# Two-layer hybrid attention kernel: normalised x behind the last attention tile's casts, the last output tile in another PSUM bank, and seven scheduling constants

## The chip, the cores and the metric

The kernel runs on one core of a Trainium2 chip. The core has five engines that work side by side, each through its own queue in order: TensorE (PE, matmuls), VectorE (DVE), ScalarE (ACT), GpSimd (POOL) and SyncE (SP, which here only issues DMAs). They wait for one another through semaphores. Time is device microseconds of one execution; several executions are run and the median counts. All of the data is float32, and matmuls take it in a form called fp32r.

## The reference, cut to what matters

Two layers work on 1024 latent tokens and 256 context tokens of width 1024. Each one normalises x, scales and shifts it by a modulation, projects it, mixes it, and adds the gated projection back to x.

```python
for i in range(DEPTH):                       # DEPTH = 2
    sh_l, sc_l, g_l = modulation(c, mod_w[i], mod_b[i])
    h_lat = rms_norm(x_lat, norm_g[i]) * (1.0 + sc_l[:, None, :]) + sh_l[:, None, :]
    if i % 2 == 0:   # global attention (8 heads) and windowed attention (8 heads), silu gates, @ w_out
        y_lat, y_ctx = even_mixer(...)
    else:            # conformer convolution and 2-D neighbourhood attention (8 heads, bias table), @ w_out
        y_lat, y_ctx = odd_mixer(...)
    x_lat = x_lat + g_l[:, None, :] * y_lat
return rms_norm(x_lat, final_g)
```

## The kernel before

**Splits.** A float32 matmul is made of three fp32r products of a high and a low part: `mm3` (L362) issues hi·hi, lo·hi and hi·lo. `split` (L332) makes the parts: ACT casts the high part (L334), and POOL, or DVE where asked, subtracts to give the low part (L337). So each projection is a run of PE rows on L363, L364 and L365, and each operand costs a cast and a subtraction.

**Attention** is one generator, `attn_gen` (L453), used by both layers. Its work list has *groups* (in the first layer 4 sets of heads by 10 query blocks, in the second 16 pairs of head and half), and a group has *tiles* of 128 keys. A tile is: scores on PE into a bank `st` (L531, L535), exp on ACT into `pf` (L543; in the second layer most tiles add a bias table on DVE first, L540, then exp at L541), the split of `pf` into `ph` and `pl`, and three matmuls into the group's output bank `ov` (L472, L473, L474). The tag `ov` has one PSUM bank, so the first L472 of a group must wait until DVE has read the former group's output: two transposes (L482) and two multiplies (L700 in the first layer, L1546 in the second). Every `vshare`-th split gives its subtraction to DVE instead of POOL: `VS0 = 12` in the first layer, `VSH = 5` in the second.

Before a group's scores can start, its *prep* finds the row maxima: matmuls into `mx` banks (two of them; L645, L657, L665 in the first layer, L1520, L1528 in the second), a maximum on DVE, and a transpose (`trn`, L429) that gives the rows of `QL`. Prep number i+2 begins at the start of group i: it loads Q, and its steps are traced from `LEAD` tiles later on. In the second layer a new head's keys `KAt` (768 KB, L403) are loaded at the start of the head before, into the buffer that the head before that has just left.

**Fillers.** `weave` (L563) runs attention steps and, between them, steps of a second generator that keeps PE busy: the projections of the next set of heads, then its gates, then the output projection `po`. `NFILL`, `O1` and the literal counts say how many filler steps go with how many attention steps; `LAG` ties a filler to the scores of a tile some places back. The scheduler then orders each engine's instructions by priority and by its own estimate of when operands are ready, so a constant moves rows far from where it stands.

**The end of the first layer.** `through_attention` runs beside the last group's tiles: the output projection of the middle 512 tokens (`final_proj(1)`), and the first half of its normalisation `norm_h(1)`. `make_h` (L346) then takes, for each of eight 128-row pieces dk, x·scale·rstd on DVE (L351, rstd comes from PSUM as `bc`), and a high and a low part. Where the letter of `HV` for this piece is `v`, ACT adds the shift and rounds (L354) and DVE makes the low part (L355, `hl<-x,modT,hh`); where it is `g`, ACT adds the shift (L357) and casts (L334), and POOL subtracts (L337). After the attention come the projections of the context tokens (`po<-hc`, evicted on DVE at L1185) and the rest of the other chunk's, then the second layer's first projection.

**The second layer** has the convolution and its layer norm first, then the attention, with four fillers in turn: two head projections (`p`), the first half of the output projection (`po<-oc`, whose operands `oc` are split in `out1_alloc`, L1592, by DVE as `OCE` says), a quarter more of it (`po<-od`), and the last part with the final norm.

## Time and profile before

| | us |
|---|---|
| median of 3 runs | 1495.62 (1493.93 to 1496.02) |
| the profiled execution | 1491.75, of which span 1490.0 |
| PE busy | 1419.0 |
| DVE busy | 1069.9 |
| POOL busy | 821.8 |
| ACT busy | 739.1 |

A busy share is an average over stages. PE carries most of this span, so what can be won is in the stretches where PE stands still, and which instruction it stands before.

### The profile page before, as it was taken

What the parts mean: (1) busy time and instruction counts of PE and PEld (TensorE: products, weight loads), DVE (VectorE), ACT (ScalarE), POOL (GpSimd) and SP (SyncE); (2) the same over time, 40 slices, a digit from 0 to 9 for tenths busy, and PEclk for the clock granted to TensorE, in tenths of its full rate; (3) what the DMA queues carried; (4) which work ended last, traced back from release to release, by engine and by line L of the source; (5) the groups of instructions that cost most, each with busy time, mean ns of one, the idle gap of its engine ahead of it and who ended that gap; (6) DMA issues with size and microseconds to landing.
All of it is one profiled execution on the core that took longest, in us unless ns stands there. A gap on an engine that the chain in (4) does not pass through costs nothing.

```text
span 1490.0 us, 22025 instructions
## 1 busy us (share of the span) xinstructions
PE 1419.0 (95%) x7014; PEld 1146.4 (77%) x7014; DVE 1069.9 (72%) x2126; ACT 739.1 (50%) x1537; POOL 821.8 (55%) x802
## 2 busy tenths in 40 slices
PE   7899999999999999999999989999999999999996
PEld 2898978887888777677887768888777878777775
DVE  4687676588858786667756767999838566668757
ACT  3641453646355765665444645443434354545563
POOL 3561463657456786676554755764544343254673
PEclk9899999999999999999999999999999999999998
DMA  9675145314531235452221221214495867787623
GB/s 351 209 219 164 47 134 177 96 57 151 177 93 36 82 96 161 154 174 85 91 74 45 84 98 58 84 59 121 147 312 178 234 203 223 239 258 226 197 63 120
DMA packets 182922, 215.22 MB, mean 144 GB/s; under 512 B 17292, under 2 KB 136280, under 8 KB 182808
## 3 DMA queue, kind: packets, MB, share of 16 engines
q1 hardware_dynamic: 172560, 195.97, 42.2%
q10 hardware_dynamic: 10248, 17.87, 3.9%
q8 instruction: 55, 0.90, 0.3%
q14 instruction: 59, 0.48, 0.1%
HBM read 151.64 MB, written 62.13 MB: 143 GB/s over the span
## 4 chain that ended last, share of the span: by engine, by line
PE 74%; DVE 8%; DMA 7%; issue 4%; POOL 4%; ACT 2%; SPq 0%; DVEq 0%; POOLq 0%; ACTq 0%
PE p L363 7%; PE p L365 7%; PE p L364 7%; PE ov L472 4%; PE ov L474 4%; PE st L531 4%; PE ov L473 4%; PE st L535 4%; PE po L363 4%; PE po L365 3%; PE po L364 3%; PE pq L365 3%; PE pq L363 3%; PE pq L364 3%; PE pg L363 2%
## 5 line engine op out<-in xcount | busy, mean ns | idle before, releaser
L337 POOL TENSOR_TENSOR pl<-pf,ph 128x512 fp32r<-128x512 f32 (+3 forms) x321 | 391.6, 1235 | 263.8 <-ACT ph L334 213.4
L337 POOL TENSOR_TENSOR wl<-wr,wh 128x256 fp32r<-128x256 f32 (+2 forms) x253 | 193.9, 786 | 136.9 <-ACT wh L334 105.7
L543 ACT ACTIVATE pf<-st 128x512 f32<-128x512 f32 x284 | 165.6, 597 | 158.9 <-PE st L535 141.6
L334 ACT CAST ph<-pf 128x512 fp32r<-128x512 f32 (+3 forms) x364 | 204.3, 579 | 18.2 <-PE ov L473 8.6
L363 PE MATMUL p<-hh,wh 128*128 128x512 f32 x448 | 176.7, 396 | 3.5 <-ACT vT L1405 1.4
L364 PE MATMUL p<-hl,wh 128*128 128x512 f32 x448 | 177.2, 397 | 0.0
L365 PE MATMUL p<-hh,wl 128*128 128x512 f32 x448 | 174.2, 398 | 0.1
L334 ACT CAST wh<-wr 128x256 fp32r<-128x256 f32 (+2 forms) x260 | 100.8, 404 | 135.0 <-DMA wr<-in_od_d_dram 31.9
L472 PE MATMUL ov<-ph,Vt 128*97 128x512 f32 (+4 forms) x364 | 138.4, 381 | 12.7 <-DVE y L700 4.2
L474 PE MATMUL ov<-pl,Vt 128*97 128x512 f32 (+3 forms) x364 | 138.4, 381 | 5.2 <-POOL pl L337 2.6
L531 PE MATMUL st<-QH,KAt 128*128 128x512 f32 (+3 forms) x364 | 139.7, 385 | 2.5 <-ACT pf L543 0.9
L473 PE MATMUL ov<-ph,Vt 128*64 128x512 f32 (+3 forms) x364 | 135.9, 373 | 0.0
L535 PE MATMUL st<-QL,KBt 68*128 68x512 f32 (+3 forms) x364 | 134.6, 378 | 1.2 <-DVE QL L430 1.2
L658 DVE TENSOR_REDUCE mp<-mx 128x1 f32<-128x512 f32 x128 | 86.0, 683 | 57.6 <-PE mx L657 57.0
L1296 DVE SCALAR_TENSOR_TENSOR cps<-U,taps,cps 128x512 f32<-128x512 f32 x184 | 124.4, 747 | 0.0
L363 PEld LDWEIGHTS p<-hh,wh 128*128 128x128 f32 x448 | 84.2, 188 | 23.1 <-ACT wh L334 2.0
L365 PEld LDWEIGHTS p<-hh,wl 128*128 128x128 f32 x448 | 84.2, 188 | 20.7 <-POOL wl L337 1.0
L364 PEld LDWEIGHTS p<-hl,wh 128*128 128x128 f32 x448 | 84.2, 188 | 20.0 <-issue 0.5
L363 PE MATMUL pq<-wh,hh 128*128 128x384 f32 x256 | 88.6, 346 | 1.1 <-ACT pc L923 1.1
L365 PE MATMUL pq<-wh,hl 128*128 128x384 f32 x256 | 87.8, 344 | 1.8 <-POOL hl L337 1.8
L364 PE MATMUL pq<-wl,hh 128*128 128x384 f32 x256 | 88.3, 345 | 0.0
L472 PEld LDWEIGHTS ov<-ph,Vt 128*97 128x97 f32 (+1 forms) x364 | 60.9, 167 | 32.4 <-issue 8.2
(300 smaller groups left out, 3413.4 us busy)
## 6 DMA issues: line engine op xcount, KB each, us to landing
mw<-in_mod_w_dram SPq DMA_DIRECT2D x28, 512.0 KB, 5.9
Q<-qs SPq DMA_DIRECT2D x40, 256.0 KB, 2.7
QH<-Q SPq DMA_DIRECT2D x80, 128.0 KB, 2.8
bm<-in_d_bm_dram SPq DMA_DIRECT2D x16, 540.0 KB, 5.6
wr<-in_od_d_dram SPq DMA_DIRECT2D x64, 128.0 KB, 2.6
wr<-in_ev_qkv_dram SPq DMA_DIRECT2D x32, 192.0 KB, 4.5
QD<-spq SPq DMA_DIRECT2D x48, 128.0 KB, 2.5
KAt<-KD SPq DMA_DIRECT2D x8, 768.0 KB, 7.5
```

The source lines that it names most:

```text
L334: SC.copy(hi, src)
L337: (GP if leng == "g" else VE).tensor_tensor(lo, src, hi.bitcast(F32), op=ALU.subtract)
L363: PE.matmul(o, lh, rh, start=first, stop=False)
L364: PE.matmul(o, lh, rl, start=False, stop=False)
L365: done[0] = PE.matmul(o, ll, rh, start=False, stop=last)
L472: PE.matmul(o[0:m], V[:, vo + 64 : vo + 64 + m], ph, start=(t == 0), stop=False)
L473: PE.matmul(cut(g.ov[0:64], q0, n), V[:, vo : vo + 64], ph, start=False, stop=False)
L474: pvs.append(PE.matmul(o[0 : VW - 64], V[:, vo + 64 : vo + VW], pl, start=False, stop=(last and g.sink is None)))
L531: sts.append(PE.matmul(sf, KA[:, cs], cut(g.QH, q0, n), start=True, stop=False))
L535: PE.matmul(sf, KB[0:68, cs], cut(g.QL[0:68], q0, n), start=False, stop=True)
L543: SC.activation(pf[:, :n], st[:, :n], AF.Exp, scale=1.0 if g.bias else SCALE)
L1296: VE.scalar_tensor_tensor(pc, uc, w, pc, op0=ALU.mult, op1=ALU.add)
```

## The change

- `make_h` is cut in two. In the second layer's middle chunk, the high and low parts of pieces dk 5, 6 and 7 are issued behind the casts of the last attention tile: on each engine behind the last `cast` that it did there (ACT's `ph`, DVE's `pl`, POOL's `pl`). The order x·scale·rstd (L351) isn't bound.
- The first layer's last group takes its output bank from the tag `mx` (two banks) instead of `ov` (one).
- `HV` for the second layer: in the middle chunk piece 3 goes from g to v and piece 4 from v to g; in the last chunk piece 5 goes from v to g.
- `NFILL[2]` 34 to 37: the last set's projection runs ahead by three filler steps in 34. `O1[1]` 134 to 137: the first output projection is spread over three more attention steps, and the end of the layer has three fewer.
- `VSH` 5 to 7: a group of the second layer has seven tiles, so DVE now makes the low part of the last tile of every group, and no other.
- `OCE` v to g: the eight `oc` subtractions go from DVE to POOL.
- `LAG` (0, 0, 6, 12) to (0, 0, 3, 18). `LEAD` for the second layer 4 to 7, which delays the traced steps of a prep by three tiles.
- `AHEAD` 3 to 4 and `XA` 4 to 8: the function that `AHEAD` calls is empty in both layers, and with either value of either constant the instruction order is the same.

```diff
-LEAD = (3, 4)
-AHEAD = 3
+LEAD = (3, 7)
+AHEAD = 4
-VSH = 5
+VSH = 7
-OCE, ODE, OHE = ('v', 'g', 'g')
+OCE, ODE, OHE = ('g', 'g', 'g')
-LAG = (0, 0, 6, 12)
+LAG = (0, 0, 3, 18)
-NFILL = (34, 34, 34)
-HV = (('gggvvvvg',) * 3, ('gggvvvvg', 'vvvgvvvg', 'gggvvvvg'))
-O1 = (6, 134, 14)
+NFILL = (34, 34, 37)
+HV = (('gggvvvvg',) * 3, ('gggvvvvg', 'vvvvgvvg', 'gggvvgvg'))
+O1 = (6, 137, 14)
-XA = 4
+XA = 8
...
+    cast = [None] * 3
+    tailc = [None] * 3
     def split(src, hi, lo, heng="s", leng="g"):
         if heng == "s":
-            SC.copy(hi, src)
+            cast[0] = SC.copy(hi, src)
...
-        (GP if leng == "g" else VE).tensor_tensor(lo, src, hi.bitcast(F32), op=ALU.subtract)
+        i_ = (GP if leng == "g" else VE).tensor_tensor(lo, src, hi.bitcast(F32), op=ALU.subtract)
+        cast[2 if leng == "g" else 1] = i_
...
             shift = modT[l][:, dk, cond : cond + 1]
+            bound = tailc if l == 1 and c == 1 and dk >= 5 else [None] * 3
+            with ExitStack() as cx:
+                for b_ in bound:
+                    if b_ is not None:
+                        cx.enter_context(tc.issue_after(b_.ins))
+                make_h1(l, c, dk, x, shift, h)
+
+    def make_h1(l, c, dk, x, shift, h):
             if HV[l][c][dk] == "v":
...
-                g.ov = bank("ov", nm("ov"))
+                g.ov = bank("mx" if g is groups[-1] and not layer[0] else "ov", nm("ov"))
...
             pend.append((g, t, ph, pl))
+            tailc[:] = cast
```

No row is added to PE: it has 6838 matmul rows in both programs. Three places of the new order bear on what follows. Line numbers are 3 to 13 higher in the changed kernel (L334 is L337 there, L474 is L486). In the names, the trailing number is the tile's identity.

**The end of the first layer on ACT.** `pf_9626` and `ph_9624` belong to the last attention tile, `hh_9721` is the high part of the normalised x. Before:

```order
L543 ACTIVATE pf_9614<-st_9609 128x512
L354 ACTIVATE hh_9721<-x_1825_7287,modT_91 128x512
L334 CAST ph_9612<-pf_9614 128x512
L354 ACTIVATE hh_9721<-x_1825_7287,modT_91 128x512
L543 ACTIVATE pf_9626<-st_9621 128x512
L354 ACTIVATE hh_9721<-x_1825_7287,modT_91 128x512
L357 ACTIVATE x_1825_7287<-x_1825_7287,modT_91 128x512
L334 CAST ph_9624<-pf_9626 128x512
L354 ACTIVATE hh_9721<-x_1825_7287,modT_91 128x512 x2
```

and after:

```order
L366 ACTIVATE hh_9721<-x_1825_7287,modT_91 128x512
L337 CAST ph_9600<-pf_9602 128x512
L555 ACTIVATE pf_9614<-st_9609 128x512
L366 ACTIVATE hh_9721<-x_1825_7287,modT_91 128x512 x2
L555 ACTIVATE pf_9626<-st_9621 128x512
L369 ACTIVATE x_1825_7287<-x_1825_7287,modT_91 128x512
L337 CAST ph_9612<-pf_9614 128x512
L337 CAST ph_9624<-pf_9626 128x512
L366 ACTIVATE hh_9721<-x_1825_7287,modT_91 128x512 x2
```

Before, three high parts and one shift stand ahead of the last cast; after, four and one do, but the first of them stands two tiles further ahead.

On DVE at the same place `pl_9625` is the low part of the last tile, and `r`, `y` are the reading of the group's output. Before:

```order
L351 SCALAR_TENSOR_TENSOR x_1825_7287<-x_1825_7287,gs_93,bc_9716 128x512 x8
L355 SCALAR_TENSOR_TENSOR hl_9722<-x_1825_7287,modT_91,hh_9721 128x512 x3
L337 TENSOR_TENSOR pl_9625<-pf_9626,ph_9624 128x512
L355 SCALAR_TENSOR_TENSOR hl_9722<-x_1825_7287,modT_91,hh_9721 128x512 x3
L482 STREAM_TRANSPOSE r_2468_9642<-ov_9525 64x256 x2
L700 SCALAR_TENSOR_TENSOR y_9647<-ov_9525,gt_9559 64x256 x2
L1185 SCALAR_TENSOR_TENSOR x_1818_7263<-po_9749,modT_90,x_1818_7263 128x256
```

and after:

```order
L355 SCALAR_TENSOR_TENSOR x_1825_7287<-x_1825_7287,gs_93,bc_9716 128x512 x8
L367 SCALAR_TENSOR_TENSOR hl_9722<-x_1825_7287,modT_91,hh_9721 128x512 x4
L340 TENSOR_TENSOR pl_9625<-pf_9626,ph_9624 128x512
L367 SCALAR_TENSOR_TENSOR hl_9722<-x_1825_7287,modT_91,hh_9721 128x512 x2
L494 STREAM_TRANSPOSE r_2468_9642<-ov_9513 64x256 x2
L713 SCALAR_TENSOR_TENSOR y_9647<-ov_9513,gt_9559 64x256 x2
L497 RECIPROCAL r_2469_9643<-r_2468_9642 128x8
```

One `hl` has moved from behind the last tile's subtraction to the front of it. On PE, 14 attention rows stand between the four `bc` matmuls that release this chain and the last L474 before, and 24 after.

**A change of group in the first layer's last set**, on PE. `ov_5543` and `ov_5552` are the old group's output bank, `ov_5814` and `ov_5832` the new one's. Before:

```order
L474 MATMUL ov_5543<-pl_5679,Vt_1219 97x512
L645 MATMUL mx_5810<-KAt_3656,QH_5690 128x256 x2
L429 MATMUL trn_5687<-ident,nmt_5661 4x128
L531 MATMUL st_5796<-QH_5441,KAt_3656 128x512
L657 MATMUL mx_5818<-KAt_3656,QH_5690 128x512
L472 MATMUL ov_5814<-ph_5698,Vt_1219 128x512
```

and after (`pq` is the projection of the next set):

```order
L376 MATMUL pq_6117<-wl_4970,hh_171 128x384
L658 MATMUL mx_5828<-KAt_3656,QH_5736 128x256 x2
L441 MATMUL trn_5733<-ident,nmt_5679 4x128
L377 MATMUL pq_6117<-wh_4969,hl_172 128x384
L375 MATMUL pq_6117<-wh_4975,hh_171 128x384
L376 MATMUL pq_6117<-wl_4976,hh_171 128x384
L377 MATMUL pq_6117<-wh_4975,hl_172 128x384
L543 MATMUL st_5814<-QH_5467,KAt_3656 128x512
L670 MATMUL mx_5836<-KAt_3656,QH_5736 128x512
L484 MATMUL ov_5832<-ph_5744,Vt_1219 128x512
```

With the rows ahead of these, 15 PE instructions now stand between the old group's last product and the new group's first, where there were five.

**The first maxima of a new head in the second layer**, on PE: `KAt_11736` (before) and `KAt_11737` (after) are head 3's keys, whose load can start when the last scores on the same buffer (L531, head 1) are done. Before, the stretch ends so, with `mx` last, after 18 rows of the projection `p_3352`:

```order
L474 MATMUL ov_13255<-pl_13364,Vt_12352 97x512
L363 MATMUL p_3352_13679<-hh_9721,wh_13460 128x512
L364 MATMUL p_3352_13679<-hl_9722,wh_13460 128x512
L365 MATMUL p_3352_13679<-hh_9721,wl_13461 128x512
L363 MATMUL p_3352_13679<-hh_9721,wh_13466 128x512
```

and after it ends in the maxima themselves:

```order
L486 MATMUL ov_13256<-pl_13322,Vt_12353 97x16x16
L543 MATMUL st_13405<-QH_12932,KAt_11734 128x256
L547 MATMUL st_13405<-QL_12933,KBt_11735 128x256
L484 MATMUL ov_13256<-ph_13343,Vt_12353 97x512
L485 MATMUL ov_13256<-ph_13343,Vt_12353 64x512
L486 MATMUL ov_13256<-pl_13344,Vt_12353 97x512
L543 MATMUL st_13425<-QH_12932,KAt_11734 128x384
L547 MATMUL st_13425<-QL_12933,KBt_11735 128x384
L1533 MATMUL mx_3343_13642<-KAt_11737,QH_13357 128x256 x2
```

The maxima have moved ahead of the projection rows: 30 PE instructions now stand between the last L531 on that buffer and the first maxima, where there were 47.

## Prediction

> **What bounds the kernel now.** I read the page's busy times, then a table of windows, then the waits of PE in the windows that the change touches.
>
> ```profile
> PE 1419.0 (95%) x7014; PEld 1146.4 (77%) x7014; DVE 1069.9 (72%) x2126; ACT 739.1 (50%) x1537; POOL 821.8 (55%) x802
> ...
> 493.00:693.00 200.00, 190.34 (x898) 144.40 (x897) 142.32 (x240) 118.47 (x221) 143.83 (x113) 0.99 0.44 135
> 693.00:850.00 157.00, 157.00 (x761) 124.89 (x760) 106.30 (x189) 80.32 (x157) 87.22 (x73) 1.00 0.23 72
> 850.00:875.00 25.00, 17.64 (x80) 13.10 (x79) 19.02 (x33) 13.85 (x28) 14.39 (x16) 0.86 0.04 10
> 875.00:1170.00 295.00, 288.86 (x1339) 234.58 (x1337) 227.63 (x373) 129.42 (x254) 159.33 (x176) 1.00 0.47 146
> 1170.00:1440.00 270.00, 256.37 (x1315) 206.44 (x1315) 190.56 (x463) 144.48 (x329) 131.48 (x150) 0.99 0.68 209
> 1440.00:1490.00 50.00, 38.17 (x218) 32.20 (x216) 29.99 (x70) 18.46 (x44) 25.11 (x27) 0.92 0.30 105
> ```
>
> The second column is the window's length, the third PE's busy time, the first figure behind the brackets the granted clock. PE is the bound: it does the same 6838 matmuls before and after, so only its idle time can move. The order is the same up to about 493 us. Behind that PE idles 9.7 us in the first layer's third set (200.00 - 190.34), nothing to 850, 7.4 in the 25 us at the layer's end, 6.1 in the convolution, 13.6 in the second attention, 11.8 in the tail. What PE waits for at the layer's end, and in the second attention:
>
> ```profile
> PE ov L474 <- DVE pl L337: 2.4, 1, 2.4
> PE po L363 <- ACT hh L334: 1.9, 1, 1.9
> PE po L363 <- DVE x L1185: 1.6, 1, 1.6
> ...
> PE ov L472 <- DVE yu L1546: 3.4, 2, 2.5
> PE ov L472 <- issue: 1.7, 2, 1.4
> PE mx L1520 <- DMA QH<-QD: 1.5, 1, 1.5
> ...
> PE po L363 <- ACT od L334: 1.4, 1, 1.4
> PE mx L1520 <- DMA KAt<-KD: 1.1, 2, 0.7
> ```
>
> The columns are total, times and longest. No single wait is large; the change can win some microseconds, not tens.
>
> **PE's own pace**, for what lies beside a wait: consecutive 512-wide rows start 0.235 us apart, 256-wide ones 0.12.
>
> ```profile
> 1350.09 0.40 PE L364 MATMUL po<-oc,wh 128*128 128x512 f32 x1
> 1350.32 0.40 PE L365 MATMUL po<-oc,wl 128*128 128x512 f32 x1
> ```
>
> **Term 1, the first layer's end.**
>
> ```profile
> 851.75 1.05 PE L299 MATMUL bc<-ident,nr 128*128 128x128 f32 x8
> 852.84 5.36 DVE L351 SCALAR_TENSOR_TENSOR x<-x,gs,bc 128x512 f32<-128x512 f32 x8 [4.32 <-PE bc L299]
> 858.11 2.07 DVE L355 SCALAR_TENSOR_TENSOR hl<-x,modT,hh 128x512 fp32r<-128x512 f32 x3
> 860.10 0.68 DVE L337 TENSOR_TENSOR pl<-pf,ph 128x512 fp32r<-128x512 f32 x1
> 860.70 4.11 DVE L355 SCALAR_TENSOR_TENSOR hl<-x,modT,hh 128x512 fp32r<-128x512 f32 x3
> 864.82 0.92 DVE L482 STREAM_TRANSPOSE r<-ov 64x256 f32<-64x256 f32 x2
> 865.77 0.85 DVE L700 SCALAR_TENSOR_TENSOR y<-ov,gt 64x256 f32<-64x256 f32 x2
> 866.65 1.27 DVE L1185 SCALAR_TENSOR_TENSOR x<-po,modT,x 128x256 f32<-128x256 f32 x3
> 867.84 0.19 DVE L485 RECIPROCAL r<-r 128x8 f32<-128x8 f32 x1
> ...
> 851.70 5.01 POOL L337 TENSOR_TENSOR pl<-pf,ph 128x512 fp32r<-128x512 f32 x4
> 859.52 4.08 POOL L337 TENSOR_TENSOR hl<-x,hh 128x512 fp32r<-128x512 f32 x2 [2.81 <-ACT hh L334]
> ...
> 860.84 0.74 PE L474 MATMUL ov<-pl,Vt 128*97 128x512 f32 x1 [2.38 <-DVE pl L337]
> ...
> 867.19 0.38 PE L363 MATMUL po<-hc,wh 128*128 128x256 f32 x1 [1.60 <-DVE x L1185]
> ```
>
> Count from the end of `bc`, 852.80. DVE is the chain: eight products, three `hl`, the last tile's `pl`, three more `hl`, the reading of `ov`, and only then the evictions that free the banks of `po`. PE resumes with `po` at 867.19, 14.4 us after `bc`, having done 15 attention rows (3.5 us) and 24 rows of `po` (2.8): 8.1 us lost. After the change `bc` stands ten attention rows earlier (2.35 us), because `O1` lets the projection run earlier, so PE does 25 rows (5.9) beside the same chain. DVE: eight products to 5.4, *four* `hl` at 0.69 to 8.1, `pl` to 8.8. The binding thus doesn't free the last `pl`; it puts one `hl` more ahead of it. Then two `hl` (1.4) instead of three, the reading 0.92 + 0.85, reciprocal 0.19 and the first eviction 0.42 (a third of 1.27): about 12.6. PE has done 5.9 + 2.1 by then (three `po` tiles, since `ov` now holds one of their `mx` banks), so 4.6 us are lost, 3.5 fewer.
>
> That is the good end. In the rows above the second three `hl` took 4.11 beside POOL's two, the first three 2.07 with POOL idle, while the eight products (one operand in PSUM) ran at 0.67 beside POOL's `pl`. After, the four early `hl` meet POOL's last subtraction (1.25 of the 5.01) and the two late ones meet POOL's `hl`: 1.25 and 1.4 more, so 7.3 lost and 0.8 won. The Trainium skill, "SBUF — State Buffer", section "Who interferes with whom", says that a DVE instruction with two SBUF inputs and a GpSimd instruction that reads SBUF exclude each other; by that rule the won time is the 0.8, and without it the 3.5. The 4.11 agrees with it; the 0.68 of a `pl` with two SBUF inputs beside POOL's 4.08 doesn't quite.
>
> Behind that, PE's 1.9 us wait for the last output's cast goes mostly: the changed order puts the final multiply ahead of the third eviction, about 2.2 us behind the first, and PE has 18 rows of 0.12 to do. I count 1.2 won (1.2 to 1.6). The granted clock of 0.86 over these 25 us is 7 us at half speed; about half of it lies beside the waits, the other half costs running matmuls 1.7. Shorter waits may avoid it: 0 to 1.7, taken 0.3. Sum: 2.0 to 6.8 won; I take **3.0**, nearer the end that the 4.11 row shows.
>
> **Term 2, the third set.** From here on, work and cover are counted from the new and the old order of PE at the pace above.
>
> ```profile
> PE ov L472 <- DVE y L700: 3.0, 3, 1.4
> ...
> 509.44 0.47 PE L472 MATMUL ov<-ph,Vt 128*128 128x512 f32 x1 [1.42 <-DVE y L700]
> ```
>
> A group's first product waits until DVE has read the old bank. Adding PE's work between the two to the wait gives 0.8 + 1.4 here and 2.0 to 2.8 at other changes of group, so that much cover is needed. `NFILL` brings projection rows forward: cover here goes from 0.8 to 2.65 us, and the wait with it. But the filler ends earlier, and a later change falls from 3.9 of cover to 1.4, a new wait of 0.9. With a small one gone (0.2): **0.6 won**, between 2.4 won and 1.5 lost. The last group's own change has only 1.2 us of cover after; without the other bank it would wait over a microsecond there, so the bank is what keeps `O1` free of cost.
>
> **Term 3, the second attention.**
>
> ```profile
> 1422.85 0.47 PE L472 MATMUL ov<-ph,Vt 128*128 128x512 f32 x1 [2.45 <-DVE yu L1546]
> ...
> 1346.76 0.40 PE L531 MATMUL st<-QH,KAt 128*128 128x512 f32 x1
> ...
> 1358.09 0.47 PE L1520 MATMUL mx<-KAt,QH 128*128 128x256 f32 x2 [0.69 <-DMA KAt<-KD]
> ...
> 1232.41 0.40 PE L531 MATMUL st<-QH,KAt 128*128 128x512 f32 x1
> ...
> 1232.84 0.33 SPq L403 DMA_DIRECT2D KAt<-KD  x1
> ...
> 1240.37 1.48 ACT L624 CAST KBt<-KAt 64x1536 fp32r<-64x1536 f32 x1 [3.08 <-DMA KAt<-KD]
> ...
> DMA to landing us min/median/max: 5.4/7.5/8.8
> ```
>
> Changes of group: by the same count the one at 1422.85 keeps most of its wait (cover 0.35 to 0.7), and a 1.4 (from the "issue" row) loses 0.9 as its cover grows from 1.5 to 2.2. **1.2 won** (2.4 won to 0.5 lost). `VSH` is in this: the last `pl` of each group goes to DVE, 0.68 instead of POOL's 1.25, but DVE is also who reads `ov`. The 1.5 us wait for `QH` goes: PE's work between the scores that free the buffer and the maxima grows from 7.3 to 9.5 us. **1.5 won** (0 to 1.5). The 1.4 for `od` goes: there, work grows from 5.2 to 10.5 us. **1.4 won** (0 to 1.4). The `oc` subtractions leave DVE (8 x 0.68) for POOL (8 x 1.25 = 10 us); POOL is busy 131 of 270 us and covers them. Nothing; if it comes while POOL is behind with `pl`, up to 1.5 lost, and a lighter DVE could win 1.
>
> **Against it, the key loads.** The scheduler pulls the maxima up in spite of the later `LEAD`. Work between the scores that free a key buffer and the first maxima on the new keys was 7.5, 10.0, 9.2, 13.7, 9.1, 8.5 us for the six loads, and is 8.5, 6.0, 11.0, 11.7, 7.4, 7.0. The second load was issued 0.4 us after its scores (1232.41) and landed 7.5 later; the median is 7.5 too. After the change its maxima then wait 2.0 (8.0 - 6.0). The fifth was ready 11.3 us after its scores (1346.76), with a wait of 0.69; other waits in between hide some of it now as before, so 1.6 more. The sixth waits 0.6 more than its 0.4 (8.0 - 7.0 - 0.4), the fourth perhaps 0.4. I take **3.7 lost** of these 4.6, since waits elsewhere cover a part; the bounds are 0 (loads of 5.4, issued 0.4 behind their scores) and 15 (all ready 11.3 behind them, as the fifth).
>
> **Term 4, the tail.**
>
> ```profile
> 850.01 1.02 POOL L274 TENSOR_TENSOR nr<-rbv,mhalf 128x4 f32<-128x4 f32 x1
> ```
>
> The sums of the first half's last norm have 10 PE rows ahead of their `bc` instead of 14; POOL's power between them takes 1.0 of these 2.3 us. **0.2 lost** (0 to 0.5). The other edits of the convolution and of `HV` meet a PE that is covered: nothing, 1 either way.
>
> **The sum**: -3.0 - 0.6 - 1.2 - 1.5 - 1.4 + 3.7 + 0.2 = -3.8. The profiled execution took 1491.75 (span 1490.0 and 1.75 around it), so it would take 1487.95. It was 3.9 under the median of the runs shown, 1495.62, to which the same difference applies: 1491.8.
>
> **The rivals.**
> - *The keys land early*: loads of 5.4 to 6 us, so the maxima hardly wait, and the layer's end wins its upper half, 5. Then -5 - 0.6 - 4.1 + 1 + 0.2 = -8.5: 1487.1. For it: before, the keys were awaited twice only. Against: the 7.5 median.
> - *The layer's end gives next to nothing*: DVE and POOL take turns through all of it, as in the row of 4.11, so 0.8 is won there, and the wait for the last output's cast stays since its multiply is late too. Then -0.8 - 0.6 - 4.1 + 3.7 + 0.2 = -1.6: 1494.0. Against: POOL's `pl` run ahead of ACT's casts before. This is the outcome of the Trainium skill's rule named above.
> - *The keys become the bound* (slower): if all six are ready only 11.3 us behind their scores, as the fifth was, the maxima wait 2.8, 5.3, 0.3, 0, 3.9 and 4.3, 15.5 more than the 1.1 of before; with 7.7 won elsewhere and 0.2 lost that is +8: 1503.6. For it: the fifth load. Against: the 7.5 median and the load at 1232.84. It decides from about 10.5 us of key waits on, since only then the time passes 1498.6.
> - *The change doesn't do what it says* at the layer's end, because DVE's queue ahead of the last `pl` is longer, not shorter: this lies inside the second rival.
>
> **How the numbers follow.** This kernel's runs tell about 0.2% (3 us) from no change: under 1492.6 is faster, over 1498.6 slower. The forecast has 0.44 (0.31 faster, 0.13 same), early keys 0.20 (faster), the layer's end giving nothing 0.22 (0.02 faster, 0.18 same, 0.02 slower), keys as the bound 0.14 (0.03 same, 0.11 slower). So faster 0.53, same 0.34, slower 0.13. The range reaches from the early keys' time, 1486, to 1498.5, where the key waits begin to decide; that leaves out some 0.15.
>
> **What would show it.** Right: in the 25 us around the last L474 of the first layer PE idles 3 to 5 us instead of 7.4, the last `pl` still waits for DVE behind four `hl`, and the first eviction comes earlier against `bc`; the waits for `QH` and `od` are gone; maxima wait for `KAt` at the second, fifth and sixth load. Wrong: the wait for the last `pl` is longer than 2.4 and the 7.4 doesn't shrink; or the second attention idles over 17 us, with `KAt` on top of its waits.

## The result, and the profile after

The changed kernel takes **1479.62 us** (median of 6 runs, 1475.54 to 1482.03) against 1493.41 of the kernel before in the same comparison (6 runs, 1490.16 to 1496.02): a ratio of **0.9909, interval 0.9888 to 0.9929**, some 13.8 us faster. The forecast had the direction, but a size of 3.8 us. The profiled execution took 1480.86, of which span 1478.8: 11.2 less than the span before.

First the busy times of the changed kernel, and the table of windows at the same places of the program as before (behind the window's length PE, its weight loads, DVE, ACT, POOL, each with instructions; then granted clock, DMA share, GB/s):

```profile
PE 1416.9 (96%) x7014; PEld 1148.8 (78%) x7014; DVE 1064.5 (72%) x2111; ACT 745.6 (50%) x1538; POOL 832.4 (56%) x817
...
495.00:696.00 201.00, 192.41 (x899) 146.87 (x898) 146.35 (x246) 119.95 (x221) 143.71 (x114) 0.97 0.44 135
696.00:848.00 152.00, 152.00 (x736) 120.81 (x735) 100.57 (x178) 76.13 (x144) 83.46 (x69) 1.00 0.24 74
848.00:873.00 25.00, 20.86 (x102) 16.19 (x100) 20.81 (x38) 17.13 (x35) 17.31 (x16) 0.86 0.04 11
873.00:1168.00 295.00, 289.65 (x1347) 236.11 (x1346) 226.29 (x374) 132.15 (x260) 160.93 (x180) 1.00 0.48 147
1168.00:1429.00 261.00, 250.61 (x1305) 205.15 (x1304) 183.12 (x446) 146.04 (x324) 139.99 (x163) 1.00 0.69 215
1429.00:1478.80 49.80, 38.17 (x222) 32.10 (x220) 32.45 (x73) 19.91 (x46) 25.07 (x28) 0.94 0.31 107
```

PE's idle time, length less busy, is 8.6 us in the third set (9.7 before), 4.1 at the layer's end (7.4), 5.4 in the convolution (6.1), 10.4 in the second attention (13.6) and 11.6 in the tail (11.8). The drops sum to 8.5, though the second attention's window alone became 9 us shorter. Idle time misses two things: a 512-wide row is drawn 0.40 long while the next one starts 0.23 behind it, so a wait of up to 0.17 is drawn as busy, and rows at half clock are busy too.

So from here on I also use a **loss**, worked out from the trace: for each PE row, by how much the time to the next row's start is longer than the usual distance for its shape in the kernel before. It holds waits, short waits and slow clock alike. It is 128.6 us before and 117.5 after, and the difference, 11.1, is close to that of the spans, 11.2. Stages are cut at the same counts of PE rows (2420, 3320, 4060, 4180, 5660, 6300 and 6800 from the start); the second attention falls into a first part (about 1205 to 1330 us before) and a second (to 1441).

The waits of PE in the second attention, after (columns as before):

```profile
PE mx L1533 <- DMA KAt<-KD: 4.4, 3, 2.8
PE ov L484 <- DVE nmt L431: 1.4, 1, 1.4
PE st L543 <- DVE pf L552: 1.4, 2, 1.1
PE st L543 <- ACT pf L555: 0.9, 1, 0.9
PE p L375 <- ACT wh L337: 0.6, 1, 0.6
```

In the third set (495 to 696 us), after:

```profile
PE st L543 <- ACT pf L555: 5.0, 4, 2.5
PE ov L484 <- DVE y L713: 1.7, 3, 0.9
```

There the waits for the bank fell from 3.0 to 1.7, and scores wait 5.0 for ACT in their place. In the second attention the key waits are there as forecast, 4.4 against 1.1. In this profile the waits for `QH` and `od` are gone, and of the first products' waits for DVE's reading (3.4 of `yu`, 1.7 "issue") one of 1.4 is left.

### The profile page after: what moved, and what is told of

Its sections match the earlier page's. It is cut to its first block, busy times and chain, and to the rows that moved or that the text cites. A ratio compares the mean times of both kernels' runs of the same rounds, so it can differ in the third digit from the quotient of the medians.

```text
span 1478.8 us, 22013 instructions
## 1 busy us (share of the span) xinstructions
PE 1416.9 (96%) x7014; PEld 1148.8 (78%) x7014; DVE 1064.5 (72%) x2111; ACT 745.6 (50%) x1538; POOL 832.4 (56%) x817
## 4 chain that ended last, share of the span: by engine, by line
PE 76%; DMA 8%; DVE 8%; issue 2%; ACT 2%; POOL 2%; SPq 1%; ACTq 0%; DVEq 0%; POOLq 0%
PE p L375 6%; PE p L376 6%; PE p L377 6%; PE ov L484 4%; PE ov L486 4%; PE st L547 4%; PE st L543 4%; PE ov L485 4%; PE po L375 4%; PE po L376 4%; PE po L377 4%; PE pq L375 3%; PE pq L376 3%; PE pq L377 3%; PE pg L375 2%
## 5 line engine op out<-in xcount | busy, mean ns | idle before, releaser
L340 POOL TENSOR_TENSOR pl<-pf,ph 128x512 fp32r<-128x512 f32 (+1 forms) x327 | 393.4, 1216 | 239.0 <-ACT ph L337 191.6
L337 ACT CAST ph<-pf 128x512 fp32r<-128x512 f32 (+3 forms) x364 | 206.1, 580 | 18.4 <-PE ov L485 8.3
L337 ACT CAST wh<-wr 128x256 fp32r<-128x256 f32 (+2 forms) x260 | 101.3, 404 | 135.9 <-DMA wr<-in_od_d_dram 37.9
L486 PE MATMUL ov<-pl,Vt 128*97 128x512 f32 (+3 forms) x364 | 139.3, 384 | 3.9 <-POOL pl L340 3.8
L543 PEld LDWEIGHTS st<-QH,KAt 128*128 128x128 f32 x364 | 69.4, 191 | 25.8 <-ACT pf L555 10.4
```

The lines of the kernel that those rows point to most:

```text
L337: cast[0] = SC.copy(hi, src)
L340: i_ = (GP if leng == "g" else VE).tensor_tensor(lo, src, hi.bitcast(F32), op=ALU.subtract)
L486: pvs.append(PE.matmul(o[0 : VW - 64], V[:, vo + 64 : vo + VW], pl, start=False, stop=(last and g.sink is None)))
L543: sts.append(PE.matmul(sf, KA[:, cs], cut(g.QH, q0, n), start=True, stop=False))
```

## The experiments

Each kernel was compared with the kernel before on the same chip. The table has the ratio with its interval, and the loss by stage of each run's profile.

| kernel | ratio | third set | layer's end | convolution | 2nd att., first part | second part |
|---|---|---|---|---|---|---|
| before | 1 | 19.8 | 12.5 | 15.2 | 11.5 | 16.5 |
| after, as first compared | 0.9909 (0.9888 to 0.9929) | 21.4 | 8.2 | 12.5 | 12.6 | 9.0 |
| e4_all: the whole change | 0.9887 (0.9864 to 0.9910) | 17.3 | 7.5 | 14.2 | 14.4 | 8.3 |
| e5_all: the whole change | 0.9911 (0.9890 to 0.9932) | 19.9 | 8.5 | 13.2 | 11.7 | 9.6 |
| e1_layer_end | 1.0007 (0.9991 to 1.0023) | 21.9 | 9.6 | 13.6 | 18.7 | 16.0 |
| e2_second_attention | 0.9921 (0.9901 to 0.9942) | 20.4 | 11.0 | 14.9 | 14.3 | 8.8 |
| e3_nfill | 0.9977 (0.9960 to 0.9994) | 19.2 | 9.7 | 13.6 | 14.8 | 17.1 |
| l_no_end | 0.9892 (0.9871 to 0.9913) | 19.1 | 9.7 | 13.8 | 12.7 | 11.2 |
| l_no_bind | 0.9922 (0.9903 to 0.9941) | 19.5 | 10.2 | 17.6 | 12.2 | 8.7 |
| l_no_bank | 0.9907 (0.9885 to 0.9929) | 19.3 | 8.6 | 13.7 | 12.8 | 10.2 |
| l_no_vsh | 0.9953 (0.9933 to 0.9973) | 24.6 | 8.5 | 13.8 | 15.6 | 14.7 |
| l_no_oce | 0.9939 (0.9923 to 0.9954) | 16.8 | 9.3 | 14.3 | 13.0 | 14.7 |
| l_no_lag | 0.9922 (0.9906 to 0.9938) | 18.8 | 9.5 | 13.3 | 12.6 | 11.1 |
| l_no_lead | 0.9935 (0.9915 to 0.9954) | 18.9 | 9.5 | 13.4 | 10.5 | 15.9 |
| s_vsh | 0.9969 (0.9952 to 0.9986) | 20.4 | 11.0 | 14.8 | 13.6 | 15.6 |
| s_oce | 0.9985 (0.9967 to 1.0003) | 21.4 | 11.0 | 15.7 | 16.6 | 12.7 |
| s_lead | 0.9994 (0.9978 to 1.0010) | 22.5 | 12.5 | 15.9 | 15.0 | 14.9 |
| m_first | 0.9967 (0.9951 to 0.9983) | 19.1 | 8.5 | 12.6 | 19.0 | 15.7 |
| m_none | 0.9951 (0.9933 to 0.9969) | 19.0 | 7.5 | 13.8 | 18.1 | 8.5 |
| m_mix8 | 0.9907 (0.9884 to 0.9929) | 19.0 | 8.5 | 12.7 | 12.2 | 13.9 |

One execution's loss in one stage is uncertain: the third set scatters from 16.8 to 24.6 over kernels with the same order there, and up to the third set, where all orders are the same but for 3 rows, the loss is 39.1 to 43.9. In the second part of the second attention it repeats well: 16.0 to 17.1 in three kernels with the order of before (at most 11 places of 500 differ), 8.3 to 11.2 in seven with the order of the whole change. 1 us is 0.0007 of the ratio. The granted clock is part of these losses: over both parts of the second attention it stands at 0.50 for 3.4 us in the kernel before, 0 to 3.4 in the three profiles of the whole change, but 10.2 in `e3_nfill` and 20.5 in `s_oce`; 3.4 us at 0.50 delay the rows by up to 1.7.

### Three parts apart, and the whole

`e1_layer_end` is the kernel before with the bound casts, the bank from `mx`, `HV` and `O1`; the others:

```diff
 e2_second_attention
-LEAD = (3, 4)
+LEAD = (3, 7)
-VSH = 5
+VSH = 7
-OCE, ODE, OHE = ('v', 'g', 'g')
+OCE, ODE, OHE = ('g', 'g', 'g')
-LAG = (0, 0, 6, 12)
+LAG = (0, 0, 3, 18)
 e3_nfill
-NFILL = (34, 34, 34)
+NFILL = (34, 34, 37)
```

> The first layer's end alone: casts bound, output bank from mx, HV, O1; the rest as before. The forecast's sizes: 3.0 us won there, 0.2 lost in the tail, nothing in the convolution, so 2.8 under the kernel before (ratio 0.998). Reading of the two traces: 4.2 at the layer's end and 1.5 to 2.5 in the convolution, so 5.5 to 6.5 under it (0.996). If the layer's end is most of the 13.8 us, it is 10 or more under it (0.993).

> LEAD, VSH, OCE and LAG alone. The forecast's sizes: 4.1 us won, 3.7 lost on the keys, so 0.4 under the kernel before (ratio 0.9997). Reading of the two traces: the same loss on the keys, but 10 won, so 6 to 7 under it (0.9955). In both, the maxima wait for keys some 4 us in all.

> NFILL alone. The forecast's size: 0.6 us won (2.4 won to 1.5 lost), 0.9996. Reading of the two traces, where the third set's stretch lost as much beside its new waits as it won: nothing, or 1 lost (1.0 to 1.0007).

> The whole change, again beside the others. 13.8 us under the kernel before (0.991), if that figure holds on this chip. If the parts are independent, their three differences add up to this one within 3 us; if one part needs another, the whole wins more than the sum.

The second attention alone brings 0.8%, most of the whole; `NFILL` 0.2%; the layer's end alone nothing, though its own stage shows 9.6 us of loss instead of the 11.0 to 12.5 of the kernels with the old order there. Its first part of the second attention shows why: 18.7 instead of 11.5. These are the waits there, PE's row with what it waited for, in `e1_layer_end`:

```profile
1204.67 0.47 PE L1533 MATMUL mx<-KAt,QH 128*128 128x256 f32 x2 [0.51 <-DMA QH<-QD]
1207.90 0.63 PE L1431 MATMUL trv<-ident,vT 128*128 128x128 f32 x4 [2.21 <-DVE sgd L1424]
1210.38 0.77 PE L484 MATMUL ov<-ph,Vt 128*128 128x512 f32 x1 [1.85 <-issue]
```

The wait of 2.21 for DVE isn't in the kernel before. It is in `e3_nfill` too, whose order of PE in this stage is that of `e1_layer_end` row for row and differs from the kernel before in 289 of 640 rows, although no edit of either touches the second attention. In the whole change it isn't there. Beside these waits the granted clock is 0.50 for 6.8 us in `e1_layer_end` and for 3.4 in `e3_nfill`, which is part of the 18.7 and of its distance to the 14.8 of the same order. So the edits of the first layer, made alone, push the scheduler into a worse start of the second attention; together with the other four constants the order is another, and the price isn't paid. That fits the parts, which sum to 11.7 us by their medians (0.9 lost, 9.6 and 3.0 won), where the whole took 17.0 off in that comparison.

### One constant of the second attention taken back, or made alone

Each `l_no_` kernel is the whole change with one line as before, each `s_` kernel the kernel before with one line changed:

```diff
 l_no_vsh
-VSH = 7
+VSH = 5
 l_no_oce
-OCE, ODE, OHE = ('g', 'g', 'g')
+OCE, ODE, OHE = ('v', 'g', 'g')
 l_no_lag
-LAG = (0, 0, 3, 18)
+LAG = (0, 0, 6, 12)
 l_no_lead
-LEAD = (3, 7)
+LEAD = (3, 4)
```

> The whole change with VSH back at 5. If the last low part on DVE is what shortens the changes of group in the second attention, the first products of groups wait for DVE's reading by 5 to 7 us again there and the whole is 4 to 6 us slower than the whole change, some 10 us under the kernel before (0.993). The forecast, which gave VSH no part of its own in 1.2 us for all changes of group: at most 1 us slower, 0.990.

> The whole change with the eight oc subtractions back on DVE. The forecast: nothing for it, so 0.989. If a lighter DVE in the second attention's third quarter is a cause: 1 to 3 us slower than the whole change, 0.990 to 0.991.

> The whole change with LAG back at (0, 0, 6, 12). The forecast laid the waits for QH and od (1.5 and 1.4 won) to the new distances, which LAG and LEAD set: without LAG the wait for od of 1.4 comes back and the time is 1.5 to 3 us over the whole change, 0.990 to 0.991. If LAG has no part: the same as the whole change, 0.989.

> The whole change with LEAD back at 4. The forecast: the key waits of 3.7 go, the QH wait of 1.5 comes back, so 2 us faster than the whole change, 0.987 to 0.988. If the maxima's later place is itself what takes PE's waits for DVE and QH away: 2 to 5 us slower, 0.990 to 0.992, with QH waits of over 1.5 us.

> The kernel before with VSH 7 alone. In the runs that undo VSH, OCE or LEAD, the second half of the second attention (from about 1330 to 1440 us) loses 14.7 to 15.9 us to PE's waits, as much as before (16.5), against 8.3 to 9.0 in the whole change: each of the three alone seems to take the gain away. If VSH is the cause and the others only keep the maxima from waiting, VSH alone wins 3 to 5 us (ratio 0.997 to 0.998). If the gain needs all three at once: 0.999 to 1.001.

> The kernel before with OCE on POOL alone. The forecast: nothing (1.000). If the gain of the second half is a sum of parts: 2 to 5 us won (0.997 to 0.998). If it needs all three at once: 0.999 to 1.001. PE's order in the second half differs from the kernel before in few rows here, so this run also shows what the work that left DVE is worth by itself.

> The kernel before with LEAD 7 alone. The forecast: the key waits, so 1 to 3 us slower (1.001 to 1.002). If the gain of the second half is a sum of parts: 2 to 5 us won there, 1 lost on the keys (0.997 to 1.000).

Taken back alone, `VSH`, `OCE` and `LEAD` cost 0.25 to 0.65% each against the 0.9887 to 0.9911 of the whole, `LAG` 0.1 to 0.35%, which its interval doesn't tell from nothing. Made alone, `VSH` wins 0.3% and the two others nothing that can be told from no change. So I was wrong about `OCE` (nothing) and about `LEAD` (2 us faster without it), and the gain is no sum of parts: the second part, 16.5 before and about 9 in the whole, stays at 12.7 to 15.6 with one made alone and goes back to 14.7 to 15.9 with one of the three taken back. `LAG` alone, and the whole without `NFILL`, weren't run.

`LAG` did half of what the forecast said of it. Without it, the second attention has these waits:

```profile
PE mx L1533 <- DMA QH<-QD: 2.0, 1, 2.0
PE po L375 <- ACT od L337: 1.8, 2, 1.3
```

The waits for `od` are back, though `l_no_oce` has one of 2.2 with `LAG` as in the whole. The 2.0 for `QH` isn't the 1.5 of the kernel before come back: that one stood at 1335.5 us, and its place has no wait here, nor in `l_no_lead`. The 2.0 stands before the maxima of the second key load, where `after` waits 2.8 for `KAt` and `e5_all` 1.8 for `QH`.

Part of the price of taking one back can be read from the last key load. In `after`, SP's issue, the loads that ACT issues, and the cast that waits for the keys:

```profile
1368.40 0.38 SPq L415 DMA_DIRECT2D KAt<-KD  x1
...
1369.69 0.33 ACTq L1491 DMA_DIRECT2D QH<-QD  x1
...
1373.66 1.48 ACT L637 CAST KBt<-KAt 64x1536 fp32r<-64x1536 f32 x1
```

and in `l_no_oce`, with the weights of the maxima that wait (the profile names `wr`, another load, for the end of their wait):

```profile
1366.53 0.79 SPq L415 DMA_DIRECT2D KAt<-KD  x1
1366.54 0.36 ACTq L1491 DMA_DIRECT2D QH<-QD  x1
...
1374.09 1.48 ACT L637 CAST KBt<-KAt 64x1536 fp32r<-64x1536 f32 x1 [3.65 <-DMA KAt<-KD]
1374.18 0.30 PEld L1533 LDWEIGHTS mx<-KAt,QH 128*128 128x128 f32 x2 [2.87 <-DMA wr<-in_od_wo_dram]
```

The same 768 KB take 5.3 us where ACT's `QH` load is issued 1.3 us later, and 7.6 where it is issued in the same instant. For this last load it holds over all runs: the casts come 5.0 to 6.1 us behind the issue in the eight with `QH` at least 1.1 us later, 7.6 to 8.3 in the six with `QH` within 0.4 us of the keys' issue, and 6.6 to 7.5 in the six with `QH` 0.8 to 1.3 us ahead. `l_no_vsh`, `l_no_oce`, `l_no_lead`, `m_first` and `m_mix8` are five of the six, and they wait 2.1 to 3.4 us for these keys. The Trainium skill, "DMA: Bandwidth & Descriptors", section "Queues, rings and completion order", says that SP's and ACT's transfers have rings of their own on the same 16 DMA engines, which take turns between them packet by packet; the last load's times agree with it.

But the issue time of `QH` can't be the whole cause, as the fifth load shows. In `l_no_oce`:

```profile
1335.34 0.33 SPq L415 DMA_DIRECT2D KAt<-KD  x1
1335.34 0.36 ACTq L1491 DMA_DIRECT2D QH<-QD  x1
...
1340.33 1.48 ACT L637 CAST KBt<-KAt 64x1536 fp32r<-64x1536 f32 x1 [1.82 <-DMA KAt<-KD]
```

Here `QH` is issued in the same instant too, and the cast comes 5.0 us behind. Seven runs have the fifth load so, with `QH` within 0.3 us and the cast after 4.8 to 5.3 (6.8 to 9.2 in the other runs with `QH` as near), and in five of them the last load, issued within 0.4 us of `QH`, took 7.6 to 8.2. A run with the order kept and the `QH` load moved wasn't made. That the last keys come late is shown; why they do stays open.

### What VSH does

```diff
 m_first
-            split(pf[:, :n], ph[:, :n], pl[:, :n], "s", "v" if cnt[0] % vshare == 0 else "g")
+            split(pf[:, :n], ph[:, :n], pl[:, :n], "s", "v" if cnt[0] % vshare == (1 if vshare == VSH else 0) else "g")
 m_none
-VSH = 7
+VSH = 999
```

> The whole change, but in the second attention DVE makes the low part of the first tile of each group instead of the last: as many of them on DVE, at another place. If it is the place that counts (the last low part closes the group, and only then DVE may read its bank), the second half of the second attention loses 13 to 16 us to waits as without VSH, and the time is 5 to 8 us over the whole change. If it is the number (DVE relieved of 1 in 5 for 1 in 7), it is as fast as the whole change within 2 us, 8 to 10 us lost in the second half.

> The whole change, but POOL makes every low part of the second attention (16 more of 1.25 us over 270 us, DVE 16 of 0.68 fewer). If the place of the last low part counts: 13 to 16 us lost in the second half, 5 to 8 us over the whole change. If DVE's load counts: no slower than the whole change.

Both are slower than the whole change by 0.4 to 0.6%: taking the last tile's low part from DVE costs 6.4 us without any on DVE and 8.9 with the first tile's there, in medians beside `e5_all`. The stages split it. Without any on DVE, the second part keeps its gain (8.5), and the first part loses 18.1; there PE waits for POOL's low parts and for ACT. In `m_none`, first part:

```profile
PE ov L486 <- POOL pl L340: 3.1, 3, 1.5
PE trv L1431 <- ACT vc L1413: 2.5, 1, 2.5
```

With the first low part of each group on DVE, PE waits for DVE's reading again, in the first part of `m_first`:

```profile
PE ov L484 <- DVE yu L1559: 3.7, 1, 3.7
```

Neither expectation holds whole: the number on DVE doesn't explain `m_first`, and the place doesn't explain the second part of `m_none`. The second part of `m_first` also has the late sixth keys (3.4 us), so its 15.7 isn't the place alone.

### LEAD by halves

```diff
 m_mix8
-                    work.append((x + LEAD[layer[0]], preps[k]))
+                    work.append((x + (4 if layer[0] and k < 8 else LEAD[layer[0]]), preps[k]))
```

> The whole change, with LEAD 4 for the preps 2 to 7 and 7 from prep 8 on. The key wait at the second load (2.0 to 2.8 us in all runs with LEAD 7 and the other three constants) goes as it did with LEAD 4 throughout (0.2 there), and the second half keeps its 8 to 9 us of loss, so 2 to 3 us under the whole change, faster than both kernels. Rival: the second half's gain hangs on the exact order, which changes in 220 of its 500 rows; then 11 to 16 us are lost there and the time is 1 to 5 us over the whole change.

> The whole change again, beside the three others on one chip: ratio 0.989 to 0.991, second half 8 to 9.5 us of loss, the wait for the second key load 2 to 3 us.

The second key wait shrank to 0.6 us as meant, but the first part stayed at 12.2, for a wait of 1.9 for `wh` came in its place, and the second part lost 13.9 with 2.1 at the sixth load. 0.9907 against 0.9911: no version here beats the whole change.

### The first layer's edits

`l_no_end` is the whole change without the bound casts, the other bank, `HV` and `O1`. Its order in the second attention is that of the whole change.

```diff
 l_no_bind
-            bound = tailc if l == 1 and c == 1 and dk >= 5 else [None] * 3
+            bound = [None] * 3
 l_no_bank
-                g.ov = bank("mx" if g is groups[-1] and not layer[0] else "ov", nm("ov"))
+                g.ov = bank("ov", nm("ov"))
```

> The whole change without the first layer's end (no bound casts, bank from ov, HV and O1 as before): NFILL and the second attention's four constants. Its order in the second attention is that of the whole change. The forecast's size for the layer's end, 3.0: it is 2.8 slower than the whole change, some 11 to 12 us under the kernel before (0.992). If the layer's end gives nothing, as its run alone said, it is as fast as the whole change (0.989 to 0.990).

> The whole change with the low and high parts of the last normalised pieces not bound behind the last tile's casts. The forecast held that the binding doesn't free the last low part and puts one more product ahead of it: without it the layer's end is the same within 1 us, and so is the time (0.990 to 0.992). If the binding is what wins there: PE idles 7 us in the layer's end as before instead of 4 to 5, and the time is 2 to 3 us over the whole change (0.992 to 0.993).

> The whole change with the first layer's last group in a bank of ov. The forecast: without the other bank that group's first product waits over a microsecond for the reading of the old one, some 10 us ahead of the layer's end, and nothing else changes, so 1 to 1.5 us over the whole change (0.991 to 0.992). Rival: the group's change is covered, no difference.

Without all of the layer's end the time is 0.9892, inside what the whole change gave three times. The losses say why: `NFILL` alone brings the layer's end from 11.6 (mean of the five kernels with the old order) to 9.7 and the convolution from 15.3 to 13.6, because the order changes there too; the layer's own edits bring the stage to 9.6 without `NFILL` and to 8.6 with it (mean of eleven kernels). They are worth 2.0 alone and 1.1 in company, and a difference of 1.1 can't be seen in the times.

Without the binding the last `pl` stands behind six `hl` on DVE, and PE waits 3.0 for it; in the three profiles of the whole it stands behind four and PE waits at most 0.2 for it. So the binding does bring the last `pl` forward. PE idles 5.9 us at the layer's end, where the three profiles of the whole have 4.1, 4.2 and 6.1, and the loss there is 10.2 instead of 8.6. More is lost elsewhere: the convolution loses 17.6 instead of 13.4 in this one profile, of which 3.1 before a broadcast that waits for POOL:

```profile
PE bc L299 <- POOL nr L274: 3.1, 1, 3.1
```

PE's order in the convolution changes with the binding in some 400 of 1480 places, so this price isn't the binding's own for certain.

Without the bank nothing changed (loss 8.6 at the layer's end, 1.9 ahead of it, both as in the whole change), so the rival was right: that change of group is covered either way.

## Why the prediction was right in its direction and wrong in its size

Against the kernels with the old order, the whole change's mean losses moved by -1.6 in the third set (21.1 to 19.4), -3.0 at the layer's end (11.6 to 8.6), -1.9 in the convolution, +1.4 and -7.6 in the two parts of the second attention (11.5 and 16.5 in the one profile of the kernel before, 12.9 and 8.9 in the mean of three of the whole), and about nothing in the tail (9.3 to 8.9): 13.1 together, near the 13.8 of the times.

**Term 1, the layer's end: right in size, for the most part by another road.** Forecast 3.0, measured 3.0 by loss. PE idles 4.1 us in `after` instead of 7.4, in the range given, but 6.1 in `e5_all`. In `after` the rows of DVE, of POOL and of PE:

```profile
853.09 5.36 DVE L355 SCALAR_TENSOR_TENSOR x<-x,gs,bc 128x512 f32<-128x512 f32 x8 [2.36 <-PE bc L299]
858.36 2.74 DVE L367 SCALAR_TENSOR_TENSOR hl<-x,modT,hh 128x512 fp32r<-128x512 f32 x4
861.01 0.69 DVE L340 TENSOR_TENSOR pl<-pf,ph 128x512 fp32r<-128x512 f32 x1
861.61 3.45 DVE L367 SCALAR_TENSOR_TENSOR hl<-x,modT,hh 128x512 fp32r<-128x512 f32 x2
865.07 0.92 DVE L494 STREAM_TRANSPOSE r<-ov 64x256 f32<-64x256 f32 x2
...
859.65 3.17 POOL L340 TENSOR_TENSOR pl<-pf,ph 128x512 fp32r<-128x512 f32 x1 [1.70 <-ACT ph L337]
862.79 3.40 POOL L340 TENSOR_TENSOR hl<-x,hh 128x512 fp32r<-128x512 f32 x2
...
862.88 0.74 PE L486 MATMUL ov<-pl,Vt 128*97 128x512 f32 x1 [2.54 <-POOL pl L340]
```

DVE's chain is the forecast one: eight products, four `hl` at 0.69, the last `pl`, two more. But PE no longer waits for that `pl`, so this step of the forecast failed; it waits 2.5 for the low part one tile ahead of it, on POOL, which waited 1.7 for ACT's cast and then took 3.17 instead of 1.25 beside DVE's `hl`. And the two late `hl` took 3.45 beside POOL's. I had charged the turns of DVE and POOL as 2.65 in all; here POOL alone loses 1.9 and DVE 2.1. The Trainium skill, "SBUF — State Buffer", section "Who interferes with whom", has both engines' reads exclude each other here, and these rows agree. The wait for the last output's cast (1.9) is gone, as forecast. So is that for the first eviction (1.6), which the forecast had kept; but the granted clock is 0.86 over these 25 us and PE's rows run slower there. In `e5_all`, with the clock at 1.00 and 8.5 of loss against 8.2, PE waits at that place for DVE's reading of the last output:

```profile
PE po L375 <- DVE y L713: 2.7, 1, 2.7
```

What I didn't see is that 1.9 of the 3.0 comes with `NFILL` alone. I also had the binding wrong: by itself it does bring the last `pl` forward.

**Term 2, the third set: right in sign, as far as the scatter lets one tell.** Forecast 0.6 won, measured 1.6 by loss, with a scatter of 2; `NFILL` alone took 3.0 off the median, which is 1.9 by loss in this stage, 1.9 at the layer's end and 1.6 in the convolution, less 3.9 in the second attention, within the scatter. The cover at the changes of group did its work (3.0 us of waits to 1.7).

**The convolution: priced at nothing, 1.9 won.** I put `HV` and the moved rows there beside "a PE that is covered". They may not be only covered: with the binding taken away, one profile loses over 4 more there.

**Term 3 failed.** It was -0.4 in all and is -6.2. The price of the loads was near: the waits of a new head's first maxima for keys or `QH` are 2.6 in the kernel before and 4.4, 3.0 and 3.2 in the three profiles of the whole, 0.5 to 1.8 more, where the forecast had 2.2 more (3.7 lost on keys, 1.5 won on `QH`). At the second load 2.0 were forecast, and PE waits 2.8, 2.3 and 1.8. Only in `after` is that for the keys alone: in `e4_all` they were ready 3.4 us earlier and `QH` came last, in `e5_all` `QH` landed 0.2 us behind them. At the fifth 2.3 were forecast (0.69 and 1.6 more), and it is 1.2, 0 and 0.9; the sixth wait didn't come. These rows of `after` are the second load's issue, the cast, and the maxima:

```profile
1227.13 0.43 SPq L415 DMA_DIRECT2D KAt<-KD  x1
...
1235.59 1.48 ACT L637 CAST KBt<-KAt 64x1536 fp32r<-64x1536 f32 x1 [4.37 <-DMA KAt<-KD]
...
1235.71 0.47 PE L1533 MATMUL mx<-KAt,QH 128*128 128x256 f32 x2 [2.80 <-DMA KAt<-KD]
```

The step that failed is the gain: "1.2 won" at the changes of group, with `VSH` in it, 1.5 for `QH`, 1.4 for `od`, and "Nothing" for `OCE`. The term is mis-sized: 4.1 were forecast, and the second part alone won 7.6 with the key waits already paid. `VSH` or `OCE` taken back costs 5.7 of loss there, of which some 3 are the late last keys. Loss by what PE stood before there, before and in `after`: first products 3.9 and 1.6, maxima that need keys or `QH` 3.4 and 1.4, maxima that wait for DVE 1.1 and 0, `po` on `od` 1.6 and 0.2, scores 1.1 and 2.6, everything under 0.2 us a row 5.3 and 3.2 (together 16.5 and 9.0, with 0.2 before for low parts). I priced the two named waits near enough and the rest not. Of the 7.5 won, 2.3 are at first products, 1.1 at maxima that wait for DVE and 2.1 in rows of under 0.2, and the last two weren't in the forecast at all. A change of group shrinks more than its cover tells, since the reading itself starts earlier. The old group's last product, and what DVE does up to the reading of its bank, in the kernel before:

```profile
1419.33 0.48 PE L474 MATMUL ov<-pl,Vt 128*97 128x512 f32 x1
...
1419.76 0.68 DVE L430 TENSOR_TENSOR QL<-trn,k_bd 4x512 fp32r<-4x512 f32 x1
...
1420.47 0.29 DVE L337 TENSOR_TENSOR pl<-pf,ph 128x128 fp32r<-128x128 f32 x1
...
1420.80 0.92 DVE L482 STREAM_TRANSPOSE r<-ov 64x256 f32<-64x256 f32 x2
```

and in `after`, with the last tile's low part ahead and the new group's first product behind:

```profile
1408.23 0.69 DVE L340 TENSOR_TENSOR pl<-pf,ph 128x512 fp32r<-128x512 f32 x1 [0.24 <-ACT ph L337]
...
1409.42 0.39 PE L486 MATMUL ov<-pl,Vt 128*97 128x512 f32 x1
...
1410.30 0.92 DVE L494 STREAM_TRANSPOSE r<-ov 64x256 f32<-64x256 f32 x2
...
1411.26 0.85 DVE L1559 SCALAR_TENSOR_TENSOR yu<-ov,gt 64x256 f32<-64x256 f32 x2
...
1412.36 0.47 PE L484 MATMUL ov<-ph,Vt 128*128 128x512 f32 x1 [1.42 <-DVE nmt L431]
```

DVE starts to read 0.9 us behind the last product's start instead of 1.5: before, the split of the next group's `QL` (0.68) and a low part (0.29) stood in its queue, after, the group's low part is long done. And PE has four score rows between the two products instead of two. The wait is 1.4 instead of 2.45; I had kept most of it. In `m_none`, where DVE makes no low part at all, the wait is 1.4 too, so the shorter wait doesn't need the last low part to be DVE's. How the 1.0 divides between queue and rows wasn't tried by itself. In `l_no_oce` the wait is 1.4 as well: there the loss comes back as 2.6 for the last keys and 2.2 for `od`.

**The clock** was left out of term 3, and it didn't make the difference. These are windows right behind that wait, before and after; the number ahead of the last two is the granted clock:

```profile
1423.80:1427.40 3.60, 3.60 (x14) 2.73 (x13) 3.29 (x5) 2.59 (x6) 2.16 (x2) 0.53 0.00 0
...
1412.30:1416.00 3.70, 3.41 (x19) 2.36 (x19) 3.42 (x7) 2.58 (x5) 2.06 (x2) 1.00 0.01 2
```

3.6 us at 0.53 are 1.7 lost. With the order of before, all three profiles have the clock at 0.50 behind this wait (for 3.4 to 6.8 us); with the order of the whole change, whose wait is 1.4, three of seven do (3.4 us). But where the clock stays up, PE waits a little later instead, in `after` so:

```profile
1416.90 0.50 PE L543 MATMUL st<-QH,KAt 128*128 128x512 f32 x1 [1.13 <-DVE pf L552]
```

In the 9 us behind the wait, the loss is 1.8 in the kernel before (3.5 in the two others with its order), 1.8 in `after`, and 1.8 to 2.1 in all seven, with the slow clock or without it.

**Term 4**: forecast 0.2 lost, loss 9.3 before and 8.8 to 9.1 after; nothing. **The rivals**: none came. The early keys came near for the sixth load alone, and the keys as a bound stayed away: that rival had 16.6 us of key waits, and `after` has 4.4.

## What to carry to other kernels

Where a scheduler sets the order, an edit is priced by the order it gives everywhere, not only where it is made: two edits of the first layer, each alone, lost 4 to 7 us more in the second layer's attention, by one profile each, and the whole change doesn't pay them. Parts tried one at a time can mislead, and a part should also be tried by taking it out of the whole.

Count the losses of a stage whole, start to start, short waits and clock included, before pricing single waits: what the named waits left out here was as large as they were. And compare losses, not idle time, where the clock moves: a slow clock can hide a wait that comes back when the clock stays up.

## What the runs showed of the hardware

The granted clock fell to about half behind short waits: behind one of 2.45 us in all three runs with that order, for 3.4 to 6.8 us, and behind one of 1.4 in three of seven. The Trainium skill, "TensorE: Matmul & The Clock Gate", section "Why this matters for your kernels", advises against idle gaps over about 3 us; these runs show it at half of that, not every time. Such a spell needn't cost anything: the seven profiles lost 1.8 to 2.1 us in the 9 us behind the wait of 1.4, with the slow clock or without it.

The last load of 768 KB took 5.0 to 6.1 us up to its cast where another queue's load was issued over 1 us later, and 7.6 to 8.3 where it was issued within 0.4 us. The fifth took 4.8 to 5.3 in seven runs although the other load was issued within 0.3 us, so the issue time of that one load doesn't set the duration.
